# Hybrid decoder step on one core: cumulated decays read back from DRAM into all partitions, in place of products of ones with a masked operand

## The chip, the cores and the metric

The kernel runs on one core of a Trainium2 chip. The metric is the device time of one execution in microseconds (us), as the median of several runs. The profile is that of one further execution, taken by the hardware profiler. The engines are called as in the profile: PE (TensorE matmuls), PEld (its weight loads), DVE (VectorE), ACT (ScalarE), POOL (GpSimd) and SP (SyncE, which here only issues DMAs).

## The reference

One layer of a decoder with two kinds of heads that carry a state (gated linear attention, GLA, and a state space model, SSD), cross-attention to a memory and a feed-forward part, for one prompt of 2048 tokens and for 8 samples of 4 tokens that share the weights. The change touches only the SSD heads of the prompt. Their part of the reference, for chunks of tokens and 8 heads:

```python
lc = jnp.cumsum(dtc * a_head, axis=1)                 # cumulated decays, a column for each head
seg = lc[:, :, None, :] - lc[:, None, :, :]           # lc[t] - lc[s]
decay = jnp.exp(jnp.where(causal, seg, -jnp.inf))
cb = jnp.einsum('bthn,bshn->btsh', cc, bc)
y = (jnp.einsum('btsh,bshp->bthp', cb * decay * dtc[:, None], xc)
     + jnp.einsum('bthn,bhpn->bthp', cc, s) * jnp.exp(lc)[..., None])
ll = lc[:, -1]
w = jnp.exp(ll[:, None] - lc) * dtc
s = jnp.exp(ll)[:, :, None, None] * s + jnp.einsum('bsh,bshp,bshn->bhpn', w, xc, bc)
```

For each chunk and head a matrix exp(lc[t] - lc[s]) over s (128 partitions) and t (128 columns) is needed. lc[s] is one number for each partition; lc[t] has to be there as a row, the same in all 128 partitions. How that row comes into all partitions is what the change is about.

## The kernel before

All is float32. Large products are made as three products of float32r parts (`three`, L135 to L137): high weights by high data, high by low, low by high; `wload` splits a weight into its parts on ACT (L129, `whi`) and DVE (L130, `wlo`).

The first 860 us or so hold the mixer. `block(b)` runs four times, for 512 tokens each, and a block has four chunks of 128 tokens. In a block PE works through the large products with the input weights: eight units `fm` of the convolution's columns, a narrow one (L572), then `tm(0)`, `tm(1)`, four more `fm`, and `tm(2)`. Everything of the two recurrences is written as generators and laid beside these products: `beside` is called after each unit and takes one step of the queue `side`. The order so written is not the order on the engines: the language's planner, which simulates costs, gives each engine its own order, and waits follow from the data. Each engine then takes its instructions strictly in that order.

After the narrow product, `decays()` makes softplus of the step widths on DVE (L155 to L171), multiplies by the heads' rates into `dA` (L629), and cumulates by two products: `triu` by `dA` (L632) gives `lc`, `ones` by `dA` (L633) the sums of the chunks. So `lc` has tokens on partitions and (chunk, head) on 32 columns. ACT and DVE then split `lc` into a high and a low part (`hl`, L641, L642), four transposes (L646) turn it to 16 partitions (8 heads, high and low) by 512 tokens, and DVE puts that into partitions 64 to 79 of `sp`, under the name `lcT` (L647).

For a chunk c, `ssd_first(c)` has POOL multiply the turned rows with a mask (L775): the result `R` has 16 used partitions by (8 heads, 128 tokens), where a head's row stands only in its own two partitions. Two products of a matrix of ones with `R` (L801, one for each four heads) sum over the partitions and so put lc[t] into every partition of PSUM. Eight DVE instructions (L805) take the minimum with lc[s] and subtract it, from PSUM into `M`; ACT makes the exponential of `M` (L806); DVE multiplies by the masked products `cbm` (L809, two instructions of four heads). `ssd_second(c)` multiplies `M` with the inputs (L819, eight heads, two passes each) and does the rest (L816, L821 to L831). Between the two, `ssd_first` also makes `xdt`, `xD` (DVE, L783, L785), `xw` (POOL, L787) and `Bt` (ACT, L792) from transposes (L781, L790) and the products L795.

`R` is cleared once in a block by POOL (L679); its buffer has served as scratch of the gates before (L176 to L180). There is one buffer `M`. POOL issues the DMAs of other work too (L412, L427, L440, L461, L488), in the same order as its arithmetic. After the mixer's blocks come the passes of the output projection, the cross-attention, the feed-forward part and, beside them, the samples; the change does not touch these.

Of the kernel before, what the change touches and what calls it, by code (L numbers as in the profile page):

```python
# [12 lines left out]
F32 = mybir.dt.float32  # L13
F32R = mybir.dt.float32r
# [6 lines left out]
P = 128  # L21
# [16 lines left out]
def f(ap):  # L38
    return ap.bitcast(F32)
# [3 lines left out]
def hymba_kernel(ctx: ExitStack, tc: tile.TileContext, a: dict, o: dict, dbg: dict | None = None):  # L43
# [17 lines left out]
    def mxt():  # L61
        return mx.tile([P, 512], F32, name="mx")
# [255 lines left out]
    onesr = pstate.tile([P, P], F32R, name="onesr")  # L318
    nc.vector.memset(f(onesr), 1.0)
# [19 lines left out]
    bmask = pstate.tile([P, 8], F32, name="bmask")  # L339
    nc.vector.tensor_tensor(bmask[64:80], ident[64:80, 64:72], ident[64:80, 72:80], op=ALU.add)  # L340
# [11 lines left out]
    kv = tc.dram_tile([2, 8, P, MEM], F32, name="kv")  # L352

# [173 lines left out]
    def block(b):  # L527
# [92 lines left out]
        lcT = sp[64:80]  # L620

        def decays():
            ps = mxt()
            for c in range(NCH):
                nc.tensor.transpose(ps[:, c * 8:(c + 1) * 8], sp[32:40, c * CH:(c + 1) * CH], ident[32:40, 32:40])
            softplus(dt, ps[:, 0:32], pa, P, 4)
            dA = pa.tile([P, 32], F32, name="dA")
            bc = lambda t: t.unsqueeze(1).broadcast_to([P, NCH, 8])
            nc.vector.tensor_tensor(dA.rearrange("p (c h) -> p c h", h=8), dt.rearrange("p (c h) -> p c h", h=8), bc(ahead), op=ALU.mult)  # L629
            yield  # L630
            ps = mxt()
            nc.tensor.matmul(ps[:, 0:32], lhsT=triu, rhs=dA, start=True, stop=True)  # L632
            nc.tensor.matmul(ps[:, 32:64], lhsT=ones, rhs=dA, start=True, stop=True)  # L633
            nc.vector.tensor_copy(lcl, ps[:, 0:64])
            nc.vector.tensor_tensor(wl_[:, 0:32], ll, lc, op=ALU.subtract)
            nc.vector.tensor_copy(wl_[:, 32:64], ll)
            nc.vector.tensor_copy(wl_[:, 64:96], lc)
            nc.scalar.activation(wl_, wl_, AF.Exp)
            hl = pa.tile([P, NCH, 16], F32R, name="hl")
            lc3 = lc.rearrange("p (c h) -> p c h", h=8)  # L640
            nc.scalar.activation(hl[:, :, 0:8], lc3, AF.Copy)  # L641
            nc.vector.tensor_tensor(hl[:, :, 8:16], lc3, f(hl)[:, :, 0:8], op=ALU.subtract)  # L642
            yield
            ps = mxt()
            for c in range(NCH):
                nc.tensor.transpose(ps[0:16, c * CH:(c + 1) * CH], f(hl)[:, c], ident)  # L646
            nc.vector.tensor_copy(lcT, ps[0:16])  # L647
            yield


# [6 lines left out]
        def gates():  # L657
# [20 lines left out]
            Rs.append(pa.tile([P, 8, CH], F32R, name="R"))  # L678
            nc.gpsimd.memset(f(Rs[0]), 0.0)  # L679
# [3 lines left out]
        Rs = []  # L683
# [87 lines left out]
        def ssd_first(c):  # L771
            cs = slice(c * CH, (c + 1) * CH)

            R = Rs[0]
            nc.gpsimd.tensor_tensor(out=R[64:80], in0=lcT[:, cs].unsqueeze(1).broadcast_to([16, 8, CH]),  # L775
                                    in1=bmask[64:80].unsqueeze(2).broadcast_to([16, 8, CH]), op=ALU.mult)
            M = pa.tile([P, 8, CH], F32, name="M")
# [21 lines left out]
            for g in range(2):  # L799
                pl = mxt()  # L800
                nc.tensor.matmul(pl, lhsT=onesr, rhs=R[:, 4 * g:4 * g + 4], start=True, stop=True)  # L801
                plv = pl.rearrange("p (h t) -> p h t", t=CH)
                for h in range(4):
                    s1 = lc[:, c * 8 + 4 * g + h:c * 8 + 4 * g + h + 1]
                    nc.vector.tensor_scalar(M[:, 4 * g + h], plv[:, h], s1, s1, op0=ALU.min, op1=ALU.subtract)  # L805
# [1648 lines left out]
```

## Time and profile before

| what | us |
|---|---|
| median of 3 runs | 2816.3 (2814.36 to 2820.68) |
| the profiled execution's own time | 2820.75 |
| its span from first to last instruction | 2819.0 |
| PE busy in the span | 2729.5 (97%) |
| DVE busy | 2079.1 (74%) |
| ACT busy | 1472.8 (52%) |
| POOL busy | 536.8 (19%) |
| granted clock of PE, mean | 0.991 |

A row of a timeline is: start in us from the span's start, duration in us, engine, line, operation, tiles (written <- read), shapes, how many, and in brackets how long the engine had been idle before it and what ended that. Durations of matmuls overlap: the next one starts before the profile has the last one end. So what an instruction takes of PE's time is read from one start to the next, not from the duration. A row of a group is: line, engine, operation, tiles, shapes, count | busy us, mean ns of one | idle us of the engine before them, with what ended it.

### The profile page before, as it was taken

Reading aid. Unit: us, or ns where it says so; the run is one execution under the profiler, and the core shown is the slowest. Engines: PE = TensorE matmul, PEld = TensorE weight load, DVE = VectorE, ACT = ScalarE, POOL = GpSimd, SP = SyncE. Lnnn points to the kernel's source line nnn. Section 1 sums busy time; section 2 is a strip of 40 time slices with the busy share of each in tenths; the row PEclk is TensorE's granted clock in tenths of the full one; section 3 lists DMA queues with packets and bytes.
Section 4 is the critical chain, followed back from the end, with each engine's and each line's share of the span. In section 5 each row is a group of like instructions: output and inputs, shape, how many; then the busy total and the mean of one; then the engine's idle time right before and its main releaser. Section 6 shows DMA issues by size and latency. Waiting matters only on the chain.

```text
span 2819.0 us, 41809 instructions
## 1 busy us (share of the span) xinstructions
PE 2729.5 (97%) x15207; PEld 2367.6 (84%) x15207; DVE 2079.1 (74%) x3831; ACT 1472.8 (52%) x2921; POOL 536.8 (19%) x722
## 2 busy tenths in 40 slices
PE   8999999999998999999899999999999999999998
PEld 8987888788886878878799888899998998788786
DVE  7676677776757787677888787667678878574776
ACT  5545554554546787777755434434445555353432
POOL 2142332321321321015321210001000001000011
PEclk9999999999999999999999999999999999999999
DMA  7345435343266785468864567775234436464765
GB/s 255 113 142 188 148 106 160 118 131 90 83 215 226 282 291 223 146 189 254 263 222 179 177 237 243 253 254 178 98 137 171 156 120 209 168 219 99 239 152 132
DMA packets 151102, 512.17 MB, mean 182 GB/s; under 512 B 18176, under 2 KB 29488, under 8 KB 137328
## 3 DMA queue, kind: packets, MB, share of 16 engines
q1 hardware_dynamic: 94560, 331.81, 36.0%
q0 software_dynamic: 44240, 152.82, 16.8%
q10 hardware_dynamic: 12096, 24.86, 2.7%
q8 instruction: 120, 1.97, 0.3%
q14 instruction: 86, 0.70, 0.1%
HBM read 365.76 MB, written 143.67 MB: 181 GB/s over the span
## 4 chain that ended last, share of the span: by engine, by line
PE 75%; DVE 13%; ACT 5%; DMA 3%; issue 3%; POOL 1%; DVEq 0%; ACTq 0%; SPq 0%; POOLq 0%
PE accA L135 9%; PE accA L136 9%; PE accA L137 9%; PE accC L135 5%; PE accC L136 5%; PE accC L137 5%; PE acc L135 5%; PE acc L136 5%; PE acc L137 5%; PE accB L135 2%; PE accB L137 2%; PE accB L136 2%; DVE s L1670 2%; DVE sum L1650 2%; ACT r L1739 1%
## 5 line engine op out<-in xcount | busy, mean ns | idle before, releaser
L135 PE MATMUL accA<-r,s 128*128 128x512 f32 (+2 forms) x1792 | 637.2, 356 | 19.0 <-ACT r L1739 7.2
L137 PE MATMUL accA<-r,s 128*128 128x512 f32 (+2 forms) x1792 | 629.1, 351 | 2.9 <-DVE s L1670 2.8
L136 PE MATMUL accA<-r,s 128*128 128x384 f32 (+2 forms) x1472 | 502.7, 342 | 2.4 <-DVE r L1743 2.4
L135 PEld LDWEIGHTS accA<-r,s 128*128 128x128 f32 x1792 | 339.2, 189 | 70.9 <-ACT r L1739 11.0
L1668 ACT ACTIVATE s<-sum 128x512 fp32r<-128x512 f32 (+1 forms) x456 | 282.5, 620 | 218.9 <-DVE sum L1650 105.0
L137 PEld LDWEIGHTS accA<-r,s 128*128 128x128 f32 x1792 | 339.7, 190 | 33.2 <-DVE s L1670 4.0
L135 PE MATMUL accC<-r,s 128*128 128x512 f32 (+2 forms) x896 | 318.8, 356 | 9.2 <-ACT s L1668 3.2
L1670 DVE TENSOR_TENSOR s<-sum,s 128x512 fp32r<-128x512 f32 (+1 forms) x456 | 306.8, 679 | 20.1 <-ACT s L1668 19.8
L137 PE MATMUL accC<-r,s 128*128 128x512 f32 (+2 forms) x896 | 314.3, 351 | 0.0
L136 PEld LDWEIGHTS accA<-r,s 128*128 128x128 f32 x1472 | 279.0, 190 | 19.2 <-DVE r L1743 3.6
L1670 DVE TENSOR_TENSOR s<-raw,s 128x512 fp32r<-128x512 f32 (+1 forms) x342 | 233.7, 683 | 52.0 <-ACT s L1668 50.9
L136 PE MATMUL accC<-r,s 128*128 128x384 f32 (+2 forms) x736 | 251.3, 341 | 0.5 <-DVE r L1743 0.5
L1668 ACT ACTIVATE s<-raw 128x512 fp32r<-128x512 f32 (+1 forms) x342 | 213.3, 624 | 72.1 <-PE accC L137 49.8
L129 ACT ACTIVATE whi<-wraw 128x1024 fp32r<-128x1024 f32 (+2 forms) x140 | 128.9, 934 | 184.2 <-PE acc L136 104.5
L135 PEld LDWEIGHTS accC<-r,s 128*128 128x128 f32 x896 | 169.8, 189 | 37.2 <-ACT s L1668 7.8
L130 DVE TENSOR_TENSOR wlo<-wraw,whi 128x1024 fp32r<-128x1024 f32 (+2 forms) x140 | 156.2, 1127 | 48.0 <-ACT whi L129 47.3
L137 PEld LDWEIGHTS accC<-r,s 128*128 128x128 f32 x896 | 169.7, 189 | 14.9 <-DVE s L1670 0.2
L143 POOL TENSOR_TENSOR rs<-ms,nhalf 128x1 f32<-128x1 f32 (+4 forms) x125 | 111.0, 889 | 360.3 <-DVE ms L141 343.9
L135 PE MATMUL acc<-xhl,whi 128*128 128x512 f32 (+1 forms) x464 | 168.1, 363 | 8.3 <-ACT xhl L294 8.2
L137 PE MATMUL acc<-xhl,wlo 128*128 128x512 f32 (+1 forms) x464 | 164.3, 355 | 1.7 <-DVE wlo L130 1.7
L136 PE MATMUL acc<-xhl,whi 128*128 128x512 f32 (+1 forms) x464 | 164.1, 355 | 0.2 <-DVE xhl L295 0.2
L1650 DVE TENSOR_TENSOR sum<-raw 128x512 f32<-128x512 f32 (+1 forms) x228 | 156.4, 686 | 3.6
(696 smaller groups left out, 5857.9 us busy)
## 6 DMA issues: line engine op xcount, KB each, us to landing
raw<-in_w_gu_dram SPq DMA_DIRECT2D x66, 1024.0 KB, 4.9
wraw<-in_w_in_fm_dram SPq DMA_DIRECT2D x52, 512.0 KB, 3.6
wraw<-in_w_in_tm_dram SPq DMA_DIRECT2D x48, 512.0 KB, 3.9
st<-in_w_down_dram SPq DMA_DIRECT2D x37, 512.0 KB, 6.2
aT<-og POOLq DMA_DIRECT2D x22, 768.0 KB, 4.6
raw<-aT SPq DMA_DIRECT2D x16, 1024.0 KB, 6.3
out_y_dram<-y POOLq DMA_DIRECT2D x28, 512.0 KB, 6.1
yp<-y POOLq DMA_DIRECT2D x28, 512.0 KB, 6.6
```

What stands on the lines that cost most here:

```text
L129: last[0] = nc.scalar.activation(hi[:, cs], raw[:, cs], AF.Copy)
L130: nc.vector.tensor_tensor(lo[:, cs], raw[:, cs], f(hi)[:, cs], op=ALU.subtract)
L135: nc.tensor.matmul(ps, lhsT=wh, rhs=ah, start=start, stop=False, skip_group_check=more)
L136: nc.tensor.matmul(ps, lhsT=wh, rhs=al, start=False, stop=False, skip_group_check=more)
L137: nc.tensor.matmul(ps, lhsT=wl, rhs=ah, start=False, stop=stop, skip_group_check=more)
L143: nc.gpsimd.tensor_tensor(out=rs[:rows, :cols], in0=ms[:rows, :cols], in1=nhalf[:rows, :cols], op=ALU.pow)
L1650: nc.vector.tensor_tensor(t[out], x, y, op=o)
L1668: nc.scalar.activation(h3, v, AF.Copy)
L1670: return lambda: nc.vector.tensor_tensor(l3, v, f(h3), op=ALU.subtract)
L1739: nc.scalar.activation(hi, v, AF.Copy)
```

## The change

The kernel after makes the turned decays by one product for each block: `dA` as the weights and `triu` as the moving operand give `lc` with (chunk, head) on 32 partitions and the 128 tokens of a chunk on columns. ACT copies it from PSUM into a tile `lcT`, and a DMA issued by POOL writes it to a DRAM tile `lcD`. For each chunk a second DMA, issued by POOL, reads the chunk's 8 rows of 128 numbers (4 KB) from there into all 128 partitions, straight into the tile `M`. The tile alternates between two buffers, `M` and the former `R`. The load of chunk 0 stands in a later step of `decays()`, the load of chunk c+1 at the start of `ssd_first(c)`. The eight DVE instructions then work in place on `M` in SBUF. The split of `lc`, its four transposes and their copy, the mask, the cleared `R`, POOL's product and the two products with ones are gone.

```diff
@@ setup @@
-    onesr = pstate.tile([P, P], F32R, name="onesr")
-    nc.vector.memset(f(onesr), 1.0)
+    lcT = pstate.tile([32, P], F32, name="lcT")
...
-    bmask = pstate.tile([P, 8], F32, name="bmask")
-    nc.vector.tensor_tensor(bmask[64:80], ident[64:80, 64:72], ident[64:80, 72:80], op=ALU.add)
+    pstate.tile([P, 8], F32, name="pad2")
...
+    lcD = tc.dram_tile([NB, 32, P], F32, name="lcD")
@@ decays() @@
-        lcT = sp[64:80]
...
             nc.tensor.matmul(ps[:, 32:64], lhsT=ones, rhs=dA, start=True, stop=True)
+            pt = mxt()
+            nc.tensor.matmul(pt[0:32, 0:P], lhsT=dA, rhs=triu, start=True, stop=True)
+            nc.scalar.copy(lcT, pt[0:32, 0:P])
+            nc.gpsimd.dma_start(out=lcD[b], in_=lcT)
             nc.vector.tensor_copy(lcl, ps[:, 0:64])
...
-            hl = pa.tile([P, NCH, 16], F32R, name="hl")
-            lc3 = lc.rearrange("p (c h) -> p c h", h=8)
-            nc.scalar.activation(hl[:, :, 0:8], lc3, AF.Copy)
-            nc.vector.tensor_tensor(hl[:, :, 8:16], lc3, f(hl)[:, :, 0:8], op=ALU.subtract)
-            yield
-            ps = mxt()
-            for c in range(NCH):
-                nc.tensor.transpose(ps[0:16, c * CH:(c + 1) * CH], f(hl)[:, c], ident)
-            nc.vector.tensor_copy(lcT, ps[0:16])
-            yield
-
+            yield
+            load_lc(0)
+            yield
+
+        Ms = {}
+
+        def load_lc(c):
+
+            Ms[c] = pa.tile([P, 8, CH], F32, name="MR"[c % 2])
+            nc.gpsimd.dma_start(out=Ms[c].rearrange("p h t -> p (h t)"),
+                                in_=lcD[b, 8 * c:8 * c + 8].rearrange("h t -> (h t)").unsqueeze(0).broadcast_to([P, 8 * CH]))
@@ gates() @@
-            Rs.append(pa.tile([P, 8, CH], F32R, name="R"))
-            nc.gpsimd.memset(f(Rs[0]), 0.0)
             yield
@@ ssd_first(c) @@
-            R = Rs[0]
-            nc.gpsimd.tensor_tensor(out=R[64:80], in0=lcT[:, cs].unsqueeze(1).broadcast_to([16, 8, CH]),
-                                    in1=bmask[64:80].unsqueeze(2).broadcast_to([16, 8, CH]), op=ALU.mult)
-            M = pa.tile([P, 8, CH], F32, name="M")
+            M = Ms.pop(c)
+            if c + 1 < NCH:
+                load_lc(c + 1)
...
-            for g in range(2):
-                pl = mxt()
-                nc.tensor.matmul(pl, lhsT=onesr, rhs=R[:, 4 * g:4 * g + 4], start=True, stop=True)
-                plv = pl.rearrange("p (h t) -> p h t", t=CH)
-                for h in range(4):
-                    s1 = lc[:, c * 8 + 4 * g + h:c * 8 + 4 * g + h + 1]
-                    nc.vector.tensor_scalar(M[:, 4 * g + h], plv[:, h], s1, s1, op0=ALU.min, op1=ALU.subtract)
+            for h in range(8):
+                s1 = lc[:, c * 8 + h:c * 8 + h + 1]
+                nc.vector.tensor_scalar(M[:, h], M[:, h], s1, s1, op0=ALU.min, op1=ALU.subtract)
             nc.scalar.activation(M, M, AF.Exp)
```

More of the change, by code (lines that the diff above doesn't have):

```diff
@@ L677, in gates @@
             nc.scalar.activation(bb[:, 2:4], bb[:, 2:4], AF.Exp, scale=-1.0 / 16)
-            Rs.append(pa.tile([P, 8, CH], F32R, name="R"))
-            nc.gpsimd.memset(f(Rs[0]), 0.0)
             yield
-        Rs = []
         side.append(decays())
```

## The prediction

> **What bounds the kernel now.** I read the page first: its busy shares and the chain of work that ended last.
>
> ```profile
> span 2819.0 us, 41809 instructions
> PE 2729.5 (97%) x15207; PEld 2367.6 (84%) x15207; DVE 2079.1 (74%) x3831; ACT 1472.8 (52%) x2921; POOL 536.8 (19%) x722
> PE 75%; DVE 13%; ACT 5%; DMA 3%; issue 3%; POOL 1%; DVEq 0%; ACTq 0%; SPq 0%; POOLq 0%
> ```
>
> PE is the bound of the whole, but the change lies in the four blocks, so I then asked for the busy time in blocks 1 and 2 (columns: stretch, its length, busy time of PE, PEld, DVE, ACT, POOL, clock, DMA share, GB/s).
>
> ```profile
> 332.60:512.70 180.10, 177.49 (x927) 145.17 (x927) 131.23 (x272) 88.91 (x169) 59.19 (x72) 1.00 0.44 138
> 512.70:692.80 180.10, 177.59 (x928) 145.30 (x927) 128.57 (x260) 89.03 (x169) 47.96 (x51) 1.00 0.37 110
> ```
>
> A block lasts 180.1 us and PE idles 2.5 of them; DVE is busy 71 to 73%, POOL 27 to 33%, the DMA engines about 40%. So PE's time in a block is the block's time, and what leaves PE shortens it unless PE then waits for something else. Two views say what it waits for around the change: the groups of the removed lines, and the waits.
>
> ```profile
> L801 PE MATMUL mx<-R,onesr 128*128 128x512 f32 x32 | 14.6, 477 | 4.6 <-POOL R L775 2.7 <-DVE xD L785 1.6
> L646 PE MATMUL mx<-ident,hl 128*16 128x128 f32 x16 | 2.4, 272 | 0.0
> L632 PE MATMUL mx<-dA,triu 128*128 128x32 f32 x8 | 1.6, 286 | 2.6 <-DVE dA L629 2.6
> PE mx L819 <- DVE M L809: 2.2, 4, 0.6
> ```
>
> **The change part by part.** First PE, in order of the starts (chunk 1, then chunk 0 of block 2).
>
> ```profile
> 560.38 0.48 PE L801 MATMUL mx<-R,onesr 128*128 128x512 f32 x1
> 560.70 0.40 PE L135 MATMUL acc<-whi,xhl 128*128 128x512 f32 x1
> 560.93 0.50 PE L801 MATMUL mx<-R,onesr 128*128 128x512 f32 x1
> 561.27 0.40 PE L136 MATMUL acc<-wlo,xhl 128*128 128x512 f32 x1
> ...
> 539.52 0.41 PE L632 MATMUL mx<-dA,triu 128*128 128x32 f32 x2 [0.85 <-DVE dA L629]
> 539.76 0.39 PE L633 MATMUL mx<-dA,ones 128*128 128x32 f32 x2
> 542.57 0.60 PE L646 MATMUL mx<-ident,hl 128*16 128x128 f32 x4
> 543.01 0.60 PE L781 MATMUL mx<-ident,xc 128*128 128x128 f32 x4
> 545.98 0.50 PE L801 MATMUL mx<-R,onesr 128*128 128x512 f32 x1 [0.86 <-POOL R L775]
> ```
>
> The profile's mean of 477 ns is no price, since matmuls overlap. From start to start an L801 takes 0.32 and 0.34; I take 0.32, so 0.64 a chunk. Four transposes L646 take 543.01 - 542.57 = 0.44 a block. The new product with `dA` as weights isn't in the trace; its nearest rows are L632, also float32 in two passes, 539.76 - 539.52 = 0.24 for both. Its 128 moving columns are four times theirs, which bounds it at 0.24 to 1.0 a block; the transposes L646 with 128 columns go at 0.11 each, so I take 0.24.
>
> Chunks 1 to 3 of a block lose their two L801 on PE and nothing else there, if `M` is in time. It has slack:
>
> ```profile
> 565.58 1.29 DVE L809 TENSOR_TENSOR M<-M,cbm 128x512 f32<-128x512 f32 x2
> 567.82 1.89 PE L819 MATMUL mx<-xdt,M 128*128 128x64 f32 x16
> ```
>
> L809 is done at 566.9; the first half of `M` at about 566.3, 1.5 before L819 takes it, and PE would come 0.64 sooner. So 0.9 is left, and these chunks yield 12 x 0.64 = **7.7 us**. Their loads are issued one chunk ahead, so they have the 14 us from one chunk to the next (545.98 to 560.38) for some 5; the read of chunk 2 must wait until L819 of chunk 0 has released the buffer, but POOL's older work in the queue waits for that product already (L825 by way of L823).
>
> The price of L805 changes too: it reads SBUF, not PSUM.
>
> ```profile
> L805 DVE TENSOR_SCALAR M<-mx,lcl 128x128 f32<-128x128 f32 x128 | 42.2, 402 | 2.9 <-PE mx L801 2.9
> L838 DVE TENSOR_SCALAR z<-z,rs 128x256 f32<-128x256 f32 x32 | 9.9, 351 | 12.9 <-POOL rs L143 12.9
> L775 POOL TENSOR_TENSOR R<-sp,bmask 16x1024 fp32r<-16x1024 f32 x16 | 30.7, 1920 | 34.4 <-DVE sp L647 33.0 <-PE mx L801 0.7
> 546.01 1.04 POOL L787 TENSOR_TENSOR xw<-xdt,wl__5183 128x512 f32<-128x512 f32 x1
> ```
>
> L838, the same operation in SBUF with twice the columns and one scalar fewer, takes 351 ns, so a gain of 50 ns or more each is likely (128 x 0.05 = 6 us of DVE); the other bound is that the eight wait once for POOL's L787 at 1.04 a chunk. The first is worth nothing, the second lies just over the 0.9 of slack: 0 and -12 x 0.14 = -1.7, and I take 0, as DVE idles 27 to 29%. POOL loses L775 (30.7) and gets 20 DMA issues at about 0.6 (12 us), off the path. The removed setup instructions, the cleared `R` and the split `hl` lie off PE as well: DVE and ACT have 50 and 90 us free in a block.
>
> **Chunk 0** is different: its row is on the path. Now it goes L632, L634, L641, L642, L646, L647, L775, L801. After the change it goes product, ACT copy, write, landing, read, landing. What is there to price it:
>
> ```profile
> 540.85 0.28 ACT L638 ACTIVATE wl__5183<-wl__5183 128x96 f32<-128x96 f32 x1 [1.16 <-DVE wl__5183 L637]
> 541.04 1.04 ACT L677 ACTIVATE bd<-bd 128x1024 f32<-128x1024 f32 x1
> 541.99 0.21 ACT L641 ACTIVATE hl<-lcl 128x32 fp32r<-128x32 f32 x1
> 546.40 0.37 ACT L792 COPY Bt<-mx 128x256 f32<-128x256 f32 x1
> kv<-kraw POOLq DMA_DIRECT2D x16, 128.0 KB, 2.2
> z<-in_w_xo_dram POOLq DMA_DIRECT2D x8, 512.0 KB, 4.6
> pT<-u POOLq DMA_DIRECT2D x16, 512.0 KB, 3.1
> hX<-y POOLq DMA_DIRECT2D x18, 512.0 KB, 6.9
> 546.53 2.64 DVE L805 TENSOR_SCALAR M<-mx,lcl 128x128 f32<-128x128 f32 x8 [0.99 <-PE mx L801]
> 549.21 1.06 ACT L806 ACTIVATE M<-M 128x1024 f32<-128x1024 f32 x1 [1.48 <-DVE M L805]
> 551.66 2.36 DVE L809 TENSOR_TENSOR M<-M,cbm 128x512 f32<-128x512 f32 x2
> 552.47 1.03 PE L819 MATMUL mx<-xdt,M 128*128 128x64 f32 x8
> 554.07 1.10 PE L819 MATMUL mx<-xdt,M 128*128 128x64 f32 x8 [0.57 <-DVE M L809]
> ```
>
> In block 2's times: the new product ends at 540.15 + 0.24 = 540.4; ACT is idle then (1.16 until 540.85) and copies in 0.3, between L641 and L792: 540.7. POOL has been idle; the small write from POOL lands 2.2 after its issue (the nearest is `kv`, 128 KB to DRAM): 542.9. POOL waits for that, and with it only what stands behind it, which at this place is `xw`. The read into 128 partitions of 4 KB has the form of `z<-in_w_xo`, 4.6: `M` is filled at 547.5, bounds 546.0 (3.1) and 549.8 (6.9). Then L805 2.64, L806 1.06, and L809 1.36 (two at its usual 0.68) to the 2.36 seen here: 552.6 to 553.6, middle 553.1. The second half of L819 now starts at 554.07, so 1.0 is gained. PE itself would be there at 553.50 (end of the first half) less the 0.86 waited for R, 0.64 of L801, 0.44 and plus 0.24: at 551.8. So most of what PE saves before this point it waits out at L819: **a wait takes the place of the one removed.** The early read gives 554.07 - 551.8 = 2.3; the late one with 2.36 ends at 555.9, a loss of 1.8. I take 1.0, from the row of the same shape and queue: 4 x 1.0 = **4.0** (bounds +9.2 and -7.2). The weights' parts behind L805 on DVE have several us until PE uses them, so L805 waiting 1 us at the head of DVE's queue costs no more.
>
> The 1.6 of L801 on `xD` in block 0 I leave out (0 to 1.6): it waits for DVE, which stays as loaded.
>
> Sum: 7.7 + 4.0 = 11.7. The profiled execution took 2820.75 (span 2819.0), so its like would take 2809.0; the median is 4.45 below it, and 2816.3 - 11.7 = **2804.6**.
>
> One thing in the trace speaks against issuing on POOL:
>
> ```profile
> 324.61 1.23 DVE L130 TENSOR_TENSOR wlo<-wraw,whi 128x1024 fp32r<-128x1024 f32 x1 [2.50 <-ACT whi L129]
> 324.65 1.23 POOL L590 COPY pre<-carry 128x3 f32<-128x3 f32 x1
> 329.79 0.17 POOL L590 COPY pre<-carry 128x3 f32<-128x3 f32 x1
> ```
>
> The same tiny POOL copy takes 0.17 alone and 1.23 beside a DVE instruction with operands in SBUF. If write and read are each held so at chunk 0, `M` is 2 x 1.2 = 2.4 later. [...]
>
> **The rivals.** (1) The row comes 2.4 late in chunk 0, by the held POOL just shown: 4 x 2.4 = 9.6 of 11.7 given back, 2814.2. For it: the write and the read are two issues in series. Against: POOL and DVE are both mostly idle between 540.7 and 543. (2) L819 of chunk 0 is laid later by the planner, or the read lands early, and all of PE's saving shows: 7.7 + 9.2 = 16.9, 2799.4. For it: the planner reckons with DMA times when it orders PE. (3) Slower: ACT's copy is placed behind L677 (done at 542.1), so that the row starts 1.7 later, and the read takes 6.9: filled at 551.5, L819's second half at 551.5 + 2.64 + 1.06 + 2.36 = 557.6, a loss of 3.5 a block, 14 in all, against 7.7: 2822.6. It decides from a loss of 1.9 a block, that is a fill after 549.9. For it: ACT has L638 and L677 waiting at the same place; against: the idle 1.16.
>
> **How the numbers follow.** Forecast 0.48, rival (1) 0.19, (2) 0.20, (3) 0.13. About 0.2% (5.6 us) is what a measurement of this kernel tells from no change. The forecast and (2) are faster by more: 0.68; (1) is within: 0.19; (3) slower: 0.13. The range goes from somewhat below (2), 2798 (16.9 and the 1.6 left out), to 2817, which holds (1) and a chunk 0 that gives all back; it leaves out (3).
>
> **What would show it.** L801, L646 and L775 are gone; chunks 1 to 3 show no wait of PE at L819, and a block lasts about 177. In chunk 0 the read lands 4.6 after its issue and some 7 after L633, and PE waits about 1.3 at L819 for L809, which is what the R wait was worth. Wrong would be: DVE waiting at L805 for the DMA in chunks 1 to 3; a write and read that take over 9 us together; or a block still at 180 with new idle time on PE.

## The result and the profile after

The kernel after the change takes 2798.4 us, the median of four runs (2797.70 to 2801.81), against 2815.33 for the kernel before (four runs, 2810.73 to 2820.68): a ratio of 0.9937, 95% interval [0.9925, 0.9949], so 14 to 21 us less. Run again beside fifteen runs of the kernel before, it gave 0.9944 [0.9931, 0.9956]. The forecast had the sign right, and its 11.7 us were too few: 16 to 18 were measured.

The page of the changed kernel, its span, the busy time of the engines and the chain of work that ended last:

```profile
span 2797.2 us, 41699 instructions
PE 2713.6 (97%) x15167; PEld 2357.2 (84%) x15167; DVE 2058.4 (74%) x3821; ACT 1479.8 (53%) x2927; POOL 511.1 (18%) x722
PE 76%; DVE 11%; ACT 5%; DMA 4%; issue 3%; POOL 1%; DVEq 0%; ACTq 0%; SPq 0%; POOLq 0%
```

PE is as much the bound as before. The same view of busy time by stretch for blocks 1 and 2 (from the narrow product of one block to that of the next, L571 now):

```profile
323.08:500.57 177.49, 175.26 (x919) 143.81 (x918) 129.63 (x270) 91.33 (x171) 53.13 (x72) 1.00 0.48 152
500.57:677.82 177.25, 174.95 (x919) 143.81 (x918) 125.33 (x258) 91.08 (x171) 41.60 (x51) 1.00 0.39 124
```

A block lasts 177.4 us and not 180.1, and PE idles 2.2 to 2.3 in it and not 2.5. To see the whole of what the change touches, I take the stretch from the first narrow product to the first product behind the mixer (the first `accA`). First one more profiled execution of the kernel before, then the changed kernel:

```profile
85.06:847.97 762.91, 748.36 (x4178) 619.78 (x4177) 535.06 (x1073) 382.64 (x736) 228.76 (x263) 1.00 0.44 137
```

```profile
83.73:832.39 748.66, 738.10 (x4139) 613.79 (x4137) 519.67 (x1065) 389.73 (x742) 204.62 (x263) 1.00 0.47 151
```

The stretch is 14.25 us shorter. PE's own time (its busy time) fell by 748.36 - 738.10 = **10.3**, and its waits (the rest of the stretch) fell from 14.55 to 10.56, by **4.0**. The profile that the prediction was made from gives the same waits within 0.6 (765.08 long, PE busy 749.96), but holds 1.6 us more of PE's own time, which is about what its one stretch of 3.4 us at half the clock costs. Block by block, in the same view of these two profiles, the stretch up to the second narrow product went from 244.4 to 239.4 us, the next two from 180.2 to 177.5 and from 180.1 to 177.3, and the last, up to the first `accA`, from 158.2 to 154.6. So block 0 became 5.1 us shorter, and the others 2.7, 2.9 and 3.7. The waits, in the view that groups them, of the kernel before as the prediction had it, then of the changed kernel:

```profile
PE mx L801 <- POOL R L775: 2.7, 3, 1.0
PE mx L632 <- DVE dA L629: 2.6, 3, 1.0
...
PE mx L801 <- DVE xD L785: 1.6, 1, 1.6
PE acc L136 <- DVE wlo L130: 1.5, 1, 1.5
PE mx L722 <- DVE xdt L715: 0.9, 1, 0.9
```

```profile
PE mx L629 <- DVE dA L626: 2.7, 3, 0.9
PE mx L812 <- issue: 1.6, 3, 0.6
PE acc L136 <- DVE wlo L130: 1.4, 1, 1.4
PE mx L754 <- DVE z L831: 1.0, 1, 1.0
```

Of before, the waits for `R` (2.7), for `M` at L819 (2.2, shown with the prediction), for `xD` (1.6) and for `xdt` (0.9) are gone, 7.4 in all. What is left of the wait for `M` is 1.6 at L812 (the former L819), three times and never in block 0; the view names no releaser for it ("issue"). The other waits, which the change doesn't speak of, rose by 1.8 us together (14.55 - 7.4 = 7.15, and 10.56 - 1.6 = 8.96).

### The profile page after: what moved, and what is told of

It is laid out like the page before. It is cut to its first block, busy times and chain, and to the rows that moved or that the text cites. A ratio compares the mean times of both kernels' runs of the same rounds, so it can differ in the third digit from the quotient of the medians.

```text
span 2797.2 us, 41699 instructions
## 1 busy us (share of the span) xinstructions
PE 2713.6 (97%) x15167; PEld 2357.2 (84%) x15167; DVE 2058.4 (74%) x3821; ACT 1479.8 (53%) x2927; POOL 511.1 (18%) x722
## 3 DMA queue, kind: packets, MB, share of 16 engines
q0 software_dynamic: 46672, 161.28, 17.7%
## 4 chain that ended last, share of the span: by engine, by line
PE 76%; DVE 11%; ACT 5%; DMA 4%; issue 3%; POOL 1%; DVEq 0%; ACTq 0%; SPq 0%; POOLq 0%
PE accA L135 10%; PE accA L136 10%; PE accA L137 9%; PE accC L135 5%; PE accC L136 5%; PE accC L137 5%; PE acc L135 5%; PE acc L137 5%; PE acc L136 5%; PE accB L135 3%; PE accB L137 3%; PE accB L136 2%; DVE s L1663 2%; DVE sum L1643 1%; ACT r L1732 1%
## 5 line engine op out<-in xcount | busy, mean ns | idle before, releaser
L130 DVE TENSOR_TENSOR wlo<-wraw,whi 128x1024 fp32r<-128x1024 f32 (+2 forms) x140 | 154.1, 1111 | 56.2 <-ACT whi L129 55.2
```

Of the source, the lines that this page charges most:

```text
L130: nc.vector.tensor_tensor(lo[:, cs], raw[:, cs], f(hi)[:, cs], op=ALU.subtract)
```

## The path of chunk 0 after the change

Block 2 again, from the timeline of each engine. Lines have moved: L632 is the new product, L633 ACT's copy, L634 the write, L649 the reads, L784 `xw` (L787 before), L798 the passes of DVE (L805), L799 the exponential (L806), L802 the product with `cbm` (L809), L812 the products with `M` (L819).

```profile
527.60 0.41 PE L629 MATMUL mx<-dA,triu 128*128 128x32 f32 x2 [0.86 <-DVE dA L626]
528.16 0.41 PE L632 MATMUL mx<-triu,dA 128*32 128x128 f32 x2
528.50 0.50 PE L135 MATMUL acc<-whi,xhl 128*128 128x512 f32 x1
...
528.60 0.26 ACT L633 COPY lcT<-mx 32x128 f32<-32x128 f32 x1 [0.84 <-PE mx L632]
528.76 1.05 ACT L678 ACTIVATE bd<-bd 128x1024 f32<-128x1024 f32 x1
...
529.15 0.54 POOL L634 DMA_DIRECT2D lcD<-lcT  x1 [17.01 <-ACT lcT L633]
530.78 1.04 POOL L784 TENSOR_TENSOR xw<-xdt,wl__5136 128x512 f32<-128x512 f32 x1 [1.09 <-DVE xdt L780]
531.76 0.58 POOL L649 DMA_DIRECT2D M<-lcD  x1
...
535.82 2.15 DVE L798 TENSOR_SCALAR M<-M,lcl 128x128 f32<-128x128 f32 x8 [1.62 <-DMA M<-lcD]
539.53 1.29 DVE L802 TENSOR_TENSOR M<-M,cbm 128x512 f32<-128x512 f32 x2
540.32 1.07 PE L812 MATMUL mx<-xdt,M 128*128 128x64 f32 x8 [0.45 <-issue]
541.72 1.00 PE L812 MATMUL mx<-xdt,M 128*128 128x64 f32 x8
```

To compare with the prediction's times, add 539.52 - 527.60 = 11.92, the distance of the two profiles at the product with `triu`. The row is in `M` at 535.82 + 11.92 = 547.7 (predicted 547.5), and L802 ends at 540.82 + 11.92 = 552.7 (predicted 552.6 to 553.6). So the chain over DRAM was priced well. PE is what came out another way: it waits 0.45 at L812, not 1.3. That it waits there for `M` is read from the times: half of L802 is done at about 540.2 (539.53 plus some 0.68), and L812 starts at 540.32. The DMAs, with the times of one issue on POOL and the times to landing, for the write and for the reads with it:

```profile
L634 POOL DMA_DIRECT2D lcD<-lcT x4: 514/534/579, 119.8 to 706.3; - x4
DMA to landing us min/median/max: 1.7/1.9/3.5
...
L649 POOL DMA_DIRECT2D M<-lcD x8: 570/575/583, 123.6 to 720.7; - x8
L649 POOL DMA_DIRECT2D R<-lcD x8: 541/576/631, 124.7 to 733.3; - x8
DMA to landing us min/median/max: 3.7/4.2/5.9
```

No issue took 1.2 us. And what stands in front of PE at this place, in the view by stretch for the tiles `acc` alone (the large products): from the product with `ones` to the first product with `M` in block 2, before and then after.

```profile
539.88:552.47 12.59, 9.27 (x36) 1.00 0.14 34
```

```profile
527.95:540.32 12.37, 10.01 (x40) 1.00 0.35 110
```

The planner laid four more large products there, 0.74 us of work, in blocks 1, 2 and 3 alike (36, 36, 37 before; 40, 40, 41 after). They fill more than half of the 1.3 us that the prediction had PE wait.

## The experiments

My theory after the result: (A) the gain is PE's own work, some 10 us, and waits of PE on the removed path. Rivals: (B) the gain lies behind the mixer; (C) it is VectorE's or ScalarE's lighter load; (D) the trip over DRAM has a price that is hidden or not; (E) it is the tiles of `mx` in PSUM that the removed products no longer take; (F) POOL's late issue costs something. Below, "own time" is PE's busy time and "waits" the rest of the stretch from the first narrow product to the first `accA`, both from the view by stretch of the one profiled execution. The ratio is to runs of the kernel before made beside each (medians 2815.7 to 2817.9); "before, again" is a single run.

| run | median us | ratio to before [95%] | own time | waits |
|---|---|---|---|---|
| before, again | 2815.3 | | 748.36 | 14.55 |
| after, again | 2800.3 | 0.9944 [0.9931, 0.9956] | 738.03 | 10.80 |
| ones_back | 2816.9 | 1.0003 [0.9993, 1.0012] | 750.23 | 17.80 |
| work_back | 2818.5 | 1.0006 [0.9997, 1.0014] | 748.25 | 19.48 |
| rooms_back | 2817.6 | 1.0000 [0.9991, 1.0008] | 750.73 | 13.84 |
| free_row | 2800.1 | 0.9943 [0.9930, 0.9956] | 737.54 | 11.70 |
| issue_act | 2804.2 | 0.9957 [0.9942, 0.9972] | 738.08 | 10.90 |
| prio | 2812.8 | 0.9985 [0.9975, 0.9995] | 744.40 | 20.03 |
| after_nudge | 2800.1 | 0.9947 [0.9935, 0.9960] | 738.18 | 12.32 |
| before_nudge | 2816.4 | 0.9997 [0.9988, 1.0005] | 748.07 | 14.91 |
| after_noxt | 2798.8 | 0.9939 [0.9926, 0.9951] | 738.78 | 11.85 |
| work_noxt | 2806.8 | 0.9966 [0.9955, 0.9978] | 746.88 | 11.78 |
| before_noxt | 2819.0 | 1.0013 [1.0004, 1.0022] | 748.86 | 17.67 |
| dve_back | 2809.2 | 0.9971 [0.9961, 0.9981] | 741.99 | 17.10 |
| late | 2823.8 | 1.0020 [1.0011, 1.0029] | 748.31 | 27.10 |

A stretch of 3.4 us at half the clock, where there is one, is in the own time with about 1.7 us (an estimate, half of it; the two profiles of the kernel before, one of them with such a stretch in the mixer, differ by 749.96 - 748.36 = 1.6); more on it below.

**Both kernels again, unchanged.**

> The changed kernel once more, for a narrower interval and a second profile. Theory A (PE's work plus block 0): the four blocks give 5.8 + 3 x 2.8 = 14 us, and the other 3 to 8 us between the two single profiles are stretches of half clock on PE that fall elsewhere in each execution; so the ratio comes out at 0.995 (14 us), and blocks 1 and 2 last 177.4 again. Theory B (the change also speeds up something behind the mixer): the ratio stays at 0.9937 or below (17 us or more).

> The kernel before once more, for a second profile. Theory A: blocks 1 and 2 last 180.1 again, PE waits 0.9, 0.5 and 1.6 us again in block 0, and the stretches of half clock lie at other places or are others in number. Theory B: the same places of half clock as in the first profile, since they belong to this kernel's order.

The changed kernel's own time and waits come back within 0.3 us, the stretch at half the clock of the first profile of before does not. The first `accA` starts at 833.28 and 847.97, 14.7 us apart; the spans are 16.9 apart. So most of the gain is made in the mixer, against (B). Behind it the kernel before needs 1968.3 and 1965.6 us in its two profiles, the changed one 1964.8 and 1963.4, so that some of the difference of the spans lies there.

**PE's work put back, with and without its tiles.** In ones_back each chunk gets two products into tiles of `mx` of their own, in the place of the former L801; in work_back into the tile of the transposes, so that no tile is added. Nobody reads them.

```diff
@@ ones_back: ssd_first, before the passes over M @@
+            for g in range(2):
+                pl = mxt()
+                nc.tensor.matmul(pl, lhsT=w2s[:, 0:P], rhs=sps, start=True, stop=True)
@@ work_back: ssd_first, before the transposes into px @@
+            for g in range(2):
+                nc.tensor.matmul(px, lhsT=w2s[:, 0:P], rhs=sps, start=True, stop=True)
```

> The changed kernel with two products of 96x128 weights by 512 columns, float32r, put back into each chunk behind the eight DVE instructions; nobody reads their result, so PE's work and the two PSUM rooms come back, the waits for R and the reads of DVE from PSUM do not. Theory A (what PE issues is what the mixer lasts): 32 products at 0.24 to 0.32 us, 8 to 10 us slower than the changed kernel, blocks at 179.5 to 180, block 0 still without the waits of 0.9, 0.5 and 1.6. Theory C (the gain comes from DVE, which works faster from SBUF and no longer waits for PE): under 3 us slower than the changed kernel.

> The changed kernel with the same two products put back into each chunk, but written into the room px just before the four transposes that overwrite it: PE's work comes back, no PSUM room and no reader does. In ones_back the whole gain was gone, and PE waited there for rooms (3.9 us for Bt) as well. Theory A: 32 products at 0.23 to 0.32 us each, the mixer ends 7.5 to 10 us later than in the changed kernel (832.8), that is at 840 to 843, a ratio to before of 0.997 to 0.998. Rival E (half the gain was rooms): the mixer ends 7.5 to 10 us later here, and rooms_back takes the rest. Rival C (PE's work is worth nothing, DVE or ACT pace the blocks): under 3 us later.

Both take the whole gain back, which would be too much for the work alone: work_back adds 10.2 us of own time (some 3.4 of it half clock, an estimate: half of two stretches of 3.4 us) and 8.9 of waits. The largest are waits for `z`, which the kernel before has with 0.5 us in all and the changed one with 1.0; in work_back:

```profile
PE mx L754 <- DVE z L833: 8.9, 2, 4.5
```

So these two runs do not measure what they were made for, until the waits for `z` are understood (below).

**Tiles alone.** rooms_back takes two tiles of `mx` per chunk with one tiny transpose each and a copy of 8 columns.

```diff
@@ rooms_back: ssd_first, before the passes over M @@
+            for g in range(2):
+                pl = mxt()
+                nc.tensor.transpose(pl[:, 0:8], sp[32:40, cs], ident[32:40, 32:40])
+                rj = small.tile([P, 8], F32, name="ms")
+                nc.vector.tensor_copy(rj, pl[:, 0:8])
```

> The changed kernel with the two PSUM rooms of each chunk taken again, almost without work: one 8-column transpose on PE writes each and one 8-column copy on DVE reads it, at the place where the rows were read. Theory A (rooms are worth only the 1.65 us of block 0): 2.7 us of PE for 32 small transposes at 0.085 plus at most 2, so the mixer ends 3 to 5 us later than in the changed kernel. Rival E (rooms were a part of the gain of their own): 6 us or more later, with waits of PE in chunks 1 to 3 for Bt or xD.

Here the wait comes back that the prediction had left out, PE waiting for DVE's `xD`; the groups, and one place in DVE's timeline and PE's:

```profile
PE mx L801 <- DVE xD L782: 5.0, 3, 2.3
PE mx L801 <- ACT Bt L789: 1.6, 4, 0.8
...
393.64 0.68 DVE L782 TENSOR_TENSOR xD<-mx,cols 128x512 f32<-128x512 f32 x1
394.46 0.20 PE L801 MATMUL mx<-ident,sp 8*128 8x8 f32 x1 [1.69 <-DVE xD L782]
```

The tiny transpose has no data from `xD`. What it needs is a tile of `mx`, and `xD` is the last reader of the tile of the transposes. The L801 of the kernel before has no data from `xD` either, it reads `R` and `onesr`; so its wait in block 0 was one for a free tile in PSUM, and it is gone with the two tiles per chunk: (E) holds for that part. This is shown in kind and not at the same place, since rooms_back has these waits in blocks 1, 2 and 3 (1.69, 1.03 and 2.27 us) and none in block 0. It is not the whole gain: of the 15.9 us that its stretch is longer than the changed kernel's, 12.6 are own time (1.7 of it half clock). By the price of 0.26 at one place (below), an estimate, 32 such products take 8.3 of it; what takes the rest was not followed. The profiled execution is also the shortest of its eleven runs, 5 us below their median.

**The trip over DRAM.** In free_row the reads take a row of `x`, which is there from the start, in place of the decays, so that `M` waits for no write (the decays are left out of `M`). In issue_act ACT issues the write and the reads. In late the read of chunk c is issued only at the start of chunk c, behind POOL's last instruction.

```diff
@@ free_row: load_lc @@
-                                in_=lcD[b, 8 * c:8 * c + 8].rearrange("h t -> (h t)").unsqueeze(0).broadcast_to([P, 8 * CH]))
+                                in_=a["x"][b * BT + c * CH:b * BT + c * CH + 1, :].broadcast_to([P, 8 * CH]))
@@ issue_act: decays, load_lc @@
-            nc.gpsimd.dma_start(out=lcD[b], in_=lcT)
+            nc.scalar.dma_start(out=lcD[b], in_=lcT)
...
-            nc.gpsimd.dma_start(out=Ms[c].rearrange("p h t -> p (h t)"),
+            nc.scalar.dma_start(out=Ms[c].rearrange("p h t -> p (h t)"),
@@ late: load_lc, ssd_first @@
+            behind = last_on("Pool")
-            nc.gpsimd.dma_start(out=Ms[c].rearrange("p h t -> p (h t)"),
+            d = nc.gpsimd.dma_start(out=Ms[c].rearrange("p h t -> p (h t)"),
...
+            if c:
+                keep_behind(d, behind)
...
+            if c:
+                load_lc(c)
             M = Ms.pop(c)
-            if c + 1 < NCH:
-                load_lc(c + 1)
```

> The changed kernel with the loads of the row taken from a row of the input x in place of what the block has just written: the same bytes into the same tile, but no wait for the product, its copy and the write. It leaves out the cumulated decays in M, so the outputs are not the reference's. Theory A: the row of chunk 0 is then there long before, PE's waits at the products with M (0.6, 0.4 and 0.5 us in blocks 1 to 3) go, and no more: 1 to 3 us faster than the changed kernel. Rival D (the round trip through DRAM costs more than PE's idle time shows, by the order that it forces on DVE and POOL): 5 us or more faster.

> The changed kernel with the write and the reads of the row issued by ACT in place of POOL. Theory A with what free_row showed (the row's way is hidden): within 2 us of the changed kernel; ACT waits for the landing of the write, about 1.9 us in each block. Rival F (POOL, held by DVE, makes these transfers late): 3 us or more faster.

> The changed kernel, in which the load of row c of the cumulated decays is issued at the start of chunk c (for chunks 1 to 3), behind GpSimd's last instruction issued before, and not a chunk ahead. If a trip of 3.7 to 4.2 us from issue to landing is hidden only by being issued ahead, M is late at L812 in three chunks of each block, about 1.5 to 3 us each, and the time is 20 to 35 us longer. If products of other work stand in front of L812 long enough, it is 2800 us still.

With the row free from the start, nothing is gained: 2800.1. PE's place tells why. The planner then lays L812 earlier, behind 27 large products and not 40, and PE still waits three times for `M` there, 0.8 at most:

```profile
530.06:539.80 9.74, 7.07 (x27) 1.00 0.08 30
...
PE mx L812 <- PE acc L137: 2.0, 3, 0.8
```

Issuing from ACT leaves own time and waits of the profiled execution as they are, and the median is 4 us longer than the changed kernel's; why, these runs do not show. So POOL's place for the issues (F) costs nothing that ACT's would save. But the head start is worth much. Without it, late is 24 us longer and slower than the kernel before:

```profile
PE mx L815 <- DVE R L805: 6.0, 5, 1.6
PE mx L815 <- issue: 3.8, 4, 2.4
PE acc L135 <- ACT fold L458: 3.7, 2, 2.5
...
PE mx L757 <- DVE z L834: 2.6, 2, 1.8
```

The products with `M` (L815 there) wait for it 9.8 us in nine places, other waits grow with them, and PE's own time rises by 10.2, of which five stretches of 3.4 us at half the clock are some 8.5 (an estimate, half of them; the mean clock over its 775.41 us is 0.99, where the changed kernel has 1.00). So (D): the trip costs nothing that these runs can tell while it is issued a chunk ahead and PE has other products to do, and, issued at the start of the chunk, about 24 us with all that follows from it.

**A wait named in the profile, attacked directly.** PE waits 0.9 for `dA` in three blocks, 2.7 in all, before and after. In prio the softplus and `dA` get a higher priority in the planner.

```diff
@@ prio: decays @@
-            softplus(dt, ps[:, 0:32], pa, P, 4)
+            with tc.high_priority(offset=400):
+                softplus(dt, ps[:, 0:32], pa, P, 4)
...
+            with tc.high_priority(offset=400):
                 nc.vector.tensor_tensor(dA.rearrange("p (c h) -> p c h", h=8), dt.rearrange("p (c h) -> p c h", h=8), bc(ahead), op=ALU.mult)
```

> The changed kernel with the softplus on DVE and dA placed earlier by the planner (priority raised by 400 instructions). PE's waits for dA (0.86, 0.87 and 0.95 us in blocks 1 to 3) then go and everything of chunk 0 comes sooner: 2 to 4 us faster than the changed kernel, if nothing else is pushed back. Rival: PE then waits for a split of the weights (wlo) that the softplus displaces, and the time stays.

The wait for `dA` stays at 2.6, and the kernel is 12 us longer than the changed one, with waits of L756 for `z` of 1.8 and 4.7 us. Again `z`.

**Is it the order?** Any edit lets the planner order everything behind it anew. So both kernels were run with one unread fill of one column (59 ns of DVE) in each chunk, and the changed one with eight, 8 x 59 = 472 ns, about what DVE's eight passes fell by (2.64 to 2.15 us a chunk).

```diff
@@ after_nudge, before_nudge: ssd_first, at its start @@
+            nc.vector.memset(small.tile([P, 8], F32, name="ms")[:, 0:1], 0.0)
@@ dve_back: ssd_first, at its start @@
+            ms = small.tile([P, 8], F32, name="ms")
+            for i in range(8):
+                nc.vector.memset(ms[:, i:i + 1], 0.0)
```

> The changed kernel with one unread fill of one column (128 x 1) on VectorE per chunk: no work that matters, but every instruction behind it may be placed anew by the planner. If the lengths of the blocks are the work of the change alone, the time stays at 2800 us (2797 to 2804). If the order that the planner happens to choose is worth as much as the change (the put-back runs had waits of 4 to 5 us that neither of the two kernels has), the time can be 5 to 18 us longer, with a wait of L754 for z of 4 us or more in at least one block, and the 4 us of waits that the change took away are then partly chance.

> The kernel before with one unread fill of one column per chunk on VectorE. If the order of its instructions is a matter of chance, the waits of its blocks (14.7 us up to the end of the mixer) move by some us, and with them the time: below 2812 or above 2822 us. If the waits of M, of R and of xD are its own, it stays at 2813 to 2820 us with 14 to 17 us of waits, and the changed kernel with the same fill (2800 us, 12.3 us of waits) is 14 to 18 us shorter.

> The changed kernel with eight unread fills of one column per chunk on VectorE: 8 x 59 = 472 ns, about what its eight passes over M fell by (2.64 to 2.15 us) when they read SBUF in place of PSUM. If VectorE's lighter load took the 4 us of waits away, they come back: 2803 to 2806 us, with a wait of L798 or L795 for xD in block 0. If the rooms of mx and the operand R that the change removed took them away, the time stays at 2799 to 2802 us.

One fill moves neither kernel: 2800.1 and 2816.4, own times 738.18 and 748.07, waits 12.3 and 14.9. The waits of the kernel before stay row by row. Eight fills cost 9 us, but not by the wait for `xD`, which does not come back, so VectorE's lighter load (C) is not what ended it. Of the 10.4 us that its stretch is longer than the changed kernel's, 6.5 are waits, mostly for `z` (6.8 in two places, 5.1 of it in block 2), and 3.9 are own time with three times 3.4 us at half the clock (mean clock 0.99). For the longest wait the cause can be read. The timelines of ACT and DVE of dve_back:

```profile
591.47 1.06 ACT L248 ACTIVATE xt<-xt 128x1024 f32<-128x1024 f32 x1 [5.57 <-DMA xt<-in_x_dram]
592.52 1.04 ACT L129 ACTIVATE whi<-wraw 128x1024 fp32r<-128x1024 f32 x1
...
593.60 1.23 DVE L130 TENSOR_TENSOR wlo<-wraw,whi 128x1024 fp32r<-128x1024 f32 x1 [5.19 <-ACT whi L129]
594.74 0.68 DVE L817 TENSOR_TENSOR y<-mx,wl__5208 128x512 f32<-128x512 f32 x1
...
601.69 1.09 PE L754 MATMUL mx<-ident,z 128*128 128x128 f32 x4 [5.09 <-DVE z L834]
```

and the same place in the changed kernel:

```profile
586.20 0.68 DVE L814 TENSOR_TENSOR y<-mx,wl__5136 128x512 f32<-128x512 f32 x1
...
592.08 1.23 DVE L130 TENSOR_TENSOR wlo<-wraw,whi 128x1024 fp32r<-128x1024 f32 x1 [2.16 <-ACT whi L129]
...
588.92 1.06 ACT L248 ACTIVATE xt<-xt 128x1024 f32<-128x1024 f32 x1 [5.15 <-DMA xt<-in_x_dram]
...
590.98 1.07 ACT L129 ACTIVATE whi<-wraw 128x1024 fp32r<-128x1024 f32 x1
```

In both, ACT stands 5.2 to 5.6 us at the Square of the next block's `x` (L248), which waits for its load, and the weights' part `whi` stands behind it. In the changed kernel DVE has `y`, from which `z` is made, in its queue ahead of `wlo`, so that the stall passes beside it. In dve_back `wlo` stands ahead of `y`: DVE waits 5.19 for `whi`, and `y`, `z` and PE come late. The same order (DVE idle for L130, `y` next) stands in work_back, ones_back and prio wherever they wait for `z` long.

**The stall taken away.** The next block's loads of `x` into `xt` are removed; their Squares read the identity matrix, so that these kernels leave out the statistics of the rows of blocks 1 to 3.

```diff
@@ work_noxt (on work_back), after_noxt, before_noxt: x of the next block @@
-            (nc.sync if has_s else nc.scalar).dma_start(out=xt, in_=a["x"][b * BT + i * P:b * BT + (i + 1) * P, :])
+            if has_s:
+                nc.sync.dma_start(out=xt, in_=a["x"][b * BT + i * P:b * BT + (i + 1) * P, :])
...
-            nc.scalar.activation(xt, xt, AF.Square, accum_out=ss[:, i:i + 1])
+            nc.scalar.activation(xt.rearrange("p (k c) -> p k c", c=P), xt.rearrange("p (k c) -> p k c", c=P) if has_s else ident.unsqueeze(1).broadcast_to([P, 8, P]), AF.Square, accum_out=ss[:, i:i + 1])
```

> The run with two unread products per chunk, and beside it the next block's loads of x into xt taken away: their Squares read the identity matrix, so the statistics of the rows of blocks 1 to 3 are left out. If the waits of 4.5 us of L754 for z came from ScalarE standing at its Square for those loads, they are gone in this run, and it lies 32 x 0.21 = 6.7 us above the same kernel without the two products (the run beside it), not 18. If the waits come from the planner's order for another reason, the distance stays at 15 to 18.

> The changed kernel without the next block's loads of x into xt: their Squares read the identity matrix, so the statistics of the rows of blocks 1 to 3 are left out. These loads hold nothing of PE's in the changed kernel (L754 waits 0.97 once): 2798 to 2802 us expected. If ScalarE's waits for them cost the changed kernel something too, it is 2 to 6 us shorter.

> The kernel before without the next block's loads of x into xt: their Squares read the identity matrix, so the statistics of the rows of blocks 1 to 3 are left out. If the gain of the change is PE's own work (10.2 us) and waits of its own tiles (about 4 us, of them some 2 in block 0), the distance to the changed kernel without these loads stays at 14 to 17 us. If the waits that vanished (14.7 to 10.7 us) were owed to ScalarE's place among its loads, the distance falls to 10 to 11 us.

work_noxt is 8.0 us above after_noxt (2806.8 and 2798.8), where work_back was 18 above the changed kernel; its longest wait for `z` is 0.8, and the waits of the two are 11.8 and 11.9. So two products per chunk cost 8.0 us here, 0.25 each, as own time, and the other 10 of work_back were the stall and the order. The kernel before loses nothing by these loads (without them it takes 2819.0, 3 us more than the runs beside it), nor does the changed one (2798.8 against 2800.1 with one fill). The distance of the two without them is 20 us, more than either theory had: 10.1 of own time (after_noxt has a stretch at half the clock in it, before_noxt none), 5.8 of waits, and the rest outside the mixer.

None of these kernels is faster than the changed one with the same computation.

## Why the prediction was right and wrong

**PE's work: right.** Forecast 12 x 0.64 = 7.7, and in chunk 0 0.84 a block, 11.0 in all; measured 9.9 to 10.3 (own time 748.1 to 748.4 against 738.0 to 738.2). The new product was taken at 0.24 a block and takes 528.50 - 528.16 = 0.34; that is 0.4 of the 0.8. The price of the two products has a check of its own in work_noxt: 8.0 for 32, against 32 x 0.32 = 10.2 in the prediction; other products, from other operands, so the order of size is what this confirms. In work_back the same 32 take 6.8 us of own time beside its half clock. Some 2 to 3 of the 10.3 us are therefore without a check of their own.

**Chunks 1 to 3: right in effect.** L812 waits in chunk 0 alone. One sign that the prediction had called wrong did appear: in chunk 3 DVE waits at L798 for the read (into the buffer `R`), 0.7 to 3.3 us in each block. The longest is in block 2:

```profile
561.85 0.34 DVE L798 TENSOR_SCALAR R<-R,lcl 128x128 f32<-128x128 f32 x1 [3.28 <-DMA R<-lcD]
```

But the product that needs this `M` starts at 585.46, and PE does not wait there.

**L805 in SBUF.** The passes went from 402 ns to 344 and 382 (two buffers), 42.2 to 37.9 us in all, a gain of 4.3 where 6 were worked out. The medians of the two buffers are alike, 342 and 341; the mean of 382 comes from three passes of 1.21 us, in chunk 1 of blocks 1 to 3, each beside POOL's L818 (at 544.03 in block 2, where L818 runs from 543.84 to 545.14). It looks like the wait for POOL that the prediction bounded by one in each chunk, in three chunks of sixteen; no run tests it. The passes were costed at nothing, and dve_back shows that this was too simple: half a microsecond a chunk put back on DVE cost 9 us through the order, though DVE idles more than a quarter of the time.

**Chunk 0: the row right, the wait wrong.** Copy, write, landing, read, landing and the passes ended within 0.4 of the forecast times (the write landed sooner, 1.7 after its issue and not 2.2, and the read then stood behind `xw`, as its queue had it). The step that failed is "So most of what PE saves before this point it waits out at L819: a wait takes the place of the one removed." It held the order of PE's other products fixed. The planner put four more large products in front (0.74 us), and the wait left is 0.45 to 0.6 and not 1.3. In the three blocks 1 to 3 the waits for `R` and `M` fell from 2.7 + 1.7 to 1.6; in block 0, where the first `M` comes long before its product, the 0.5 at L819 went to nothing. That is 4.9 to 1.6, a gain of 3.3 where the forecast had 4 x (1.43 - 1.3) = 0.5. The prediction had taken block 2 for all four. In blocks 1 and 2 other waits rose by most of what this gained, so that these blocks became 2.7 and 2.9 us shorter, nearly the 2.9 (1.9 + 1.0) that the forecast gives a block: there its time is right and its account of the waits is not. Most of what it lacks inside the mixer is in block 0, 5.1 us where 2.9 were forecast.

**The 1.6 of L801 on `xD`: wrong.** This is the second step that failed, a term put at nothing. "It waits for DVE, which stays as loaded" took the row's releaser for the cause. L801 reads nothing of `xD`, and rooms_back shows a wait of the same kind at a product that needs only a tile of `mx`. The change takes two such tiles per chunk away. With the 0.9 for `xdt`, also in block 0 and also gone, though no run here shows by what, this is 2.5.

**The sum.** Own time -10.3, waits for `R`, `M` -3.3, `xD` and `xdt` -2.5, other waits +1.8: -14.3, as the stretch has it. The medians differ by 16.9 and, measured again, 17.7. Some 3 us more therefore lie outside the mixer, where the profiles of each kernel wander with stretches of half clock: behind the mixer 1962.7 to 1968.3 us in the four profiles of the kernel before (as it is, with the one fill, and without the loads), 1960.3 to 1964.8 in the four of the changed one. Whether the shorter kernel meets fewer of them, these runs don't settle.

**The rivals.** Rival (2), that L819 of chunk 0 is laid later by the planner and all of PE's saving shows, is the one that came in kind: the 36 and 40 products show its mechanism. It was given 0.20, though the reason beside it, that the planner reckons with DMA times, was the better one: in free_row, where the row is there early, the planner lays L812 earlier. That its 2799.4 is 1 us from the result is partly luck. Of the 5.7 us of waits that it let go only 3.3 went, own time fell by 0.7 less, and other waits rose by 1.8; the 2.5 for `xD` and `xdt` and some 3 us outside the mixer, which it did not have, make up for that. Rival (1), a POOL held by DVE, did not come: 20 issues took 0.51 to 0.63 us. It rested on the small copy of 1.23 us; that an issue is held as that copy was is the author's assumption, no issue in this case shows such a hold, and what one would cost here is not shown either. The reads landed 3.7 to 5.9 us after their issue, and no run tells what makes this spread. Rival (3) did not come: ACT copies at 528.60, ahead of L678. But late shows that its kind of loss is real: 24 us, where the row comes late in three chunks of each block.

**The range** reached down to 2798, the 16.9 of rival (2) and the 1.6 for `xD`. The result lies at that edge, since rival (2) in part, the `xD` wait and the 3 us outside the mixer came together.

## What to carry to other kernels

Price an edit on a planned kernel first by the own time of the bounding engine: here that was good to a microsecond, while each forecast of a wait next to it was a guess at an order that the planner makes anew. A wait's named releaser may be the last reader of a buffer and not a source of data, as `xD` was for L801 in rooms_back (1.69 us); ask what the waiting instruction needs. A round trip over DRAM may cost nothing if it is issued one stage ahead, and more than it saves if it is not (2800.3 us here against 2823.8 in late, with the kernel before at 2817.2 beside it); and a put-back experiment must be read with its waits, since half a microsecond a chunk on an engine with a quarter of its time free cost 9 us here by changing who stands in front of whom.

## What the runs showed of the hardware

Around a long wait of PE the granted clock was half for a while. The stretches around the wait of 5.09 us in dve_back, which ends at 601.69 (columns as above: after the busy times of the five engines the clock, the DMA share and GB/s):

```profile
596.00:600.00 4.00, 0.59 (x3) 0.17 (x1) 1.31 (x3) 0.75 (x4) 2.42 (x2) 1.00 0.37 133
600.00:603.40 3.40, 1.71 (x6) 1.58 (x7) 1.26 (x6) 2.73 (x8) 1.72 (x2) 0.55 0.00 0
603.40:606.80 3.40, 3.40 (x9) 2.64 (x8) 1.81 (x3) 0.56 (x3) 0.00 (x0) 0.50 0.61 173
606.80:610.00 3.20, 3.20 (x15) 2.62 (x14) 0.00 (x0) 0.00 (x0) 0.00 (x0) 0.95 0.40 143
```

Nine matmuls start in 3.4 us at 0.50, against fifteen in the next 3.2. By these clocks the half clock lasts from 600.3 to 607.1, some 6.8 us (an estimate: 0.9 of the second stretch, all of the third, 0.1 of the fourth), so it begins while PE still waits; the 5.4 us of it in which PE works cost some 2.7 us (an estimate, half of them) beyond the wait itself. Apart from the last one of each, which starts behind PE's work, the traces of the kernel before and of the changed one record such stretches with 3.41, 6.83 or 10.24 us. One profile of the kernel before has such a stretch in the mixer (the clock is 0.79 from 258 to 266), the next, with 1.6 us less of own time, none; what starts and ends them, no run here tests. A product of 8 columns among large ones cost 0.15 us to its successor's start and 0.11 more behind it (556.61, 556.76, 557.10 in rooms_back, where large ones follow each other at 0.23), so 0.26 against 0.32 for 512 columns with `R`: at these two places what PE pays hardly follows the size. And a read of one row of 4 KB into 128 partitions landed 3.7 to 5.9 us after its issue, where a write of 16 KB took 1.7 to 3.5.
